# Merge gates by seven half-size products, projections after them, sigmoids and branches kept in DRAM

## The chip, the cores and the metric

The kernel runs on one core of one Trainium2 chip. The metric is device time in microseconds (us) of one execution; the kernel before has a median of 1573.55 us over three runs (1572.86 to 1573.64). The engines of the core are TensorE (PE, matrix products), VectorE (DVE), ScalarE (ACT), GpSimd (POOL) and SyncE (SP); the last two issue the DMAs here.

## What is computed

One layer of a decoder step: 512 prompt rows and 8 sample rows, model width 2048, all in float32. The reference, cut to what bears on the change:

```python
h = rmsnorm(x, norm_in_g) @ w_in          # split into q, k, v, qi, wi, ki, za, u, vb, zb, ga, gb
o_a = sparse attention over the selected keys (prompt_attention, sample_attention)
o_b, vn = gmlp_mix(u, vb, ln_g, ln_b, w_spatial, b_spatial)

def merge_out(x, o_a, z_a, o_b, z_b, g_a, g_b, w_proj_a, w_proj_b, w_out):
    y_a = (o_a * silu(z_a)) @ w_proj_a    # 1024 -> 2048
    y_b = (o_b * silu(z_b)) @ w_proj_b    # 1024 -> 2048
    mix = sigmoid(g_a) * y_a + sigmoid(g_b) * y_b
    return x + mix @ w_out                # 2048 -> 2048
# then a last rmsnorm
```

The gates g_a and g_b are each a product of h (520 x 2048) with 2048 x 2048 weights.

## The kernel before

The rows are kept turned: h is a set of 16 tiles of 128 model columns by T = 520 rows, the first 8 of them the sample rows, and each as two parts, hT_hi and hT_lo, whose sum is the float32 value. A weight is split in the same way: ACT copies it, rounded, to `whi`, and DVE subtracts that from `raw` into `wlo` (`hilo`, L127, whose two operations are at L128 and L84; nearly every DVE instruction bears the line L84 of a counting helper). PE then makes three products a weight tile, hi by hi, hi by lo, and lo by hi.

The unit of the work is a chunk: 1024 weight rows by 128 output columns. `main_chunk` (L269) issues 48 matmuls for it, eight k tiles by three products by two halves of 260 columns (HALF), into one of the two pairs of banks of `psm`, named `pm`. Output blocks over 2048 rows take two chunks, those over 1024 rows (the projections) one. A `raw` tile of 1024 rows by 256 columns (1 MB, three buffers, loaded by SP) serves two column blocks.

The loop at L1474 sets the order on every engine; nothing is reordered afterwards. In iteration i it issues the split of chunk i + 2 (LOOK), then what reads the banks of chunk i - 1 (`pending`), then the matmuls of chunk i, and then one step of every job in the list `jobs` (a job is a generator, and each `yield` ends its step for that iteration). `TT` tiles come from one pool of 37 slots.

Chunks 0 to 91 are indexer, keys, values, and the gMLP branch u, v, z_b. Then follow eight groups of four gate chunks g_b and two chunks of proj_b (92 to 139), q (140 to 155), z_a (156 to 171), gates g_a and proj_a interleaved with four blocks of lead (172 to 219), and w_out (220 to 315). A gate's `evac_g` (L1050) leaves its sigmoid `sg` in a slot, `evac_yb` (L1057) multiplies with it and stores to `mixd` in DRAM, `evac_ya` (L1319) does the same for A and adds the part of B loaded back, and `mix_split` (L1328) splits the sum into hT_hi and hT_lo, which by then no other stage reads. `oa` and `ob` are the split operands of the projections and stay in SBUF. The sample rows of `oa` come from `sample_attend` (L1154), a job of sixteen steps that starts with the last q block (L1087).

Of the kernel before, what the change touches and what calls it, by code (L numbers as in the profile page):

```python
# [38 lines left out]
GA_AHEAD = 4  # L39
NQI = T - P  # L40
WIKI_AT = 4
SEL_AT = 40
COLS_N = NS + 2 * P
# [15 lines left out]
def kernel(  # L59
# [34 lines left out]
    psm = ctx.enter_context(tc.tile_pool(name="psm", bufs=2, space=bass.MemoryType.PSUM))  # L94
    pss = ctx.enter_context(tc.tile_pool(name="pss", bufs=4, space=bass.MemoryType.PSUM))
    ctx.enter_context(tc.manual_schedule())

# [114 lines left out]
    def split_steps(i, pieces):  # L212
# [4 lines left out]
        lo = wspl.tile([P, 8, P], F32R, name="wlo")  # L217
        if ch["rows"]:
# [27 lines left out]
    def rows_chunk(ch):  # L246
        hi, lo = spl_tiles["rows", ch["kq"]]
        c = ch["c"]
        if c is None and ch["first"]:
            state["ps"] = [psm.tile([P, 2, 512], F32, name="pm") for _ in range(2)]  # L250
        elif ch["first"]:
            state["ps"] = SB("rowp")
# [16 lines left out]
    def main_chunk(i, hook=None):  # L269
        ch = chunks[i]  # L270
        if ch["rows"]:
            return rows_chunk(ch)
        if ch["first"]:
            state["ps"] = psm.tile([P, 2, 512], F32, name="pm")
# [13 lines left out]
        return ps  # L288

# [28 lines left out]
    mixd = dram.tile([KT, P, T], F32, name="mixd")  # L318

# [719 lines left out]
    def gate_b(g):  # L1039
# [4 lines left out]
        ob[g] = (TT("obh", (P, T), F32R), TT("obl", (P, T), F32R))  # L1044
        hilo(ob[g][0], ob[g][1], t)
# [30 lines left out]
    def evac_q(h):  # L1076
        def f(ps):
# [8 lines left out]
            if h == 7:  # L1086
                start(sample_attend())  # L1087
# [454 lines left out]
```

## Time and profile before

| | |
|---|---|
| median of three runs | 1573.55 us (1572.86 to 1573.64) |
| the profiled execution, its time | 1568.56 us |
| its span, first to last instruction | 1566.9 us |
| mean granted TensorE clock | 0.996 |
| PE busy | 1531.4 us, 98% |
| DVE busy | 749.3 us, 48% |
| ACT busy | 495.2 us, 32% |
| POOL busy | 262.5 us, 17% |
| DMA | 173.89 MB, mean 111 GB/s |

All rows come from one profiled execution. Busy shares are means over stages with different limits, so a stage is read by the stretch of its own. A row of a timeline gives start, duration, engine, line and operation, the output tile and after `<-` the inputs, and in brackets how long the engine had been idle and what ended that. Matmuls overlap, so the distance of their starts, not their duration, gives the pace.

### The profile page before, as it was taken

The numbers are of one execution on the slowest core, as the hardware profiler recorded it, in microseconds if no ns is written. First come the engines' busy times: TensorE is split into PE (matmuls) and PEld (weight loads), VectorE is DVE, ScalarE is ACT, GpSimd is POOL, SyncE is SP. The second block draws the span as 40 slices with busy tenths as digits, with TensorE's granted clock in tenths as the row PEclk, the third lists the DMA queues.
The fourth block names the chain that finished last, engine by engine and source line by source line (L and its number), as shares of the span: only waits on it lengthen the run. The fifth ranks groups of instructions, "written<-read, shape, count | busy, mean of one in ns | idle before, by whom it ended". The sixth has DMA issues, their size and how long they took to land. (4 is left out here: it accounts for less than half of the span.)

```text
span 1566.9 us, 28327 instructions
## 1 busy us (share of the span) xinstructions
PE 1531.4 (98%) x12222; PEld 1520.4 (97%) x12222; DVE 749.3 (48%) x1550; ACT 495.2 (32%) x803; POOL 262.5 (17%) x324
## 2 busy tenths in 40 slices
PE   5999999999999999999999999999999999999996
PEld 4999999999999999999999999999999999999996
DVE  7545447888998632222222445655223322622324
ACT  6534332433223222222212344334222222422322
POOL 3000007884000220000000002371000000410111
PEclk9999999999999999999999999999999999999998
DMA  6433224447222233332433113345223332633212
GB/s 190 137 115 103 86 88 152 162 129 179 80 83 82 84 108 99 117 95 95 125 117 110 55 55 111 106 145 166 88 89 100 117 122 88 209 99 108 81 55 110
DMA packets 147586, 173.89 MB, mean 111 GB/s; under 512 B 5876, under 2 KB 136300, under 8 KB 147452
## 3 DMA queue, kind: packets, MB, share of 16 engines
q1 hardware_dynamic: 136292, 139.74, 28.6%
q0 software_dynamic: 11168, 32.33, 6.4%
q8 instruction: 96, 1.57, 0.4%
q14 instruction: 30, 0.25, 0.0%
HBM read 162.02 MB, written 10.03 MB: 110 GB/s over the span
## 5 line engine op out<-in xcount | busy, mean ns | idle before, releaser
L285 PE MATMUL pm<-hT_hi,whi 128*128 128x260 f32 (+1 forms) x2736 | 597.4, 291 | 0.0
L285 PE MATMUL pm<-hT_lo,whi 128*128 128x260 f32 (+1 forms) x2736 | 588.7, 289 | 2.4 <-DVE hT_lo L84 2.4
L285 PE MATMUL pm<-hT_hi,wlo 128*128 128x260 f32 (+1 forms) x2720 | 584.1, 289 | 0.0
L84 DVE TENSOR_TENSOR wlo<-raw,whi 128x1024 fp32r<-128x1024 f32 (+2 forms) x260 | 325.6, 1254 | 350.4 <-ACT whi L128 349.6
L285 PEld LDWEIGHTS pm<-hT_lo,whi 128*128 128x128 f32 x2736 | 431.5, 189 | 3.5 <-DVE hT_lo L84 3.2
L285 PEld LDWEIGHTS pm<-hT_hi,whi 128*128 128x128 f32 x2736 | 431.6, 189 | 0.8
L285 PEld LDWEIGHTS pm<-hT_hi,wlo 128*128 128x128 f32 x2720 | 428.3, 189 | 0.0
L128 ACT ACTIVATE whi<-raw 128x1024 fp32r<-128x1024 f32 (+2 forms) x260 | 264.8, 1022 | 321.3 <-PE pm L285 309.9
L263 PE MATMUL pm<-hT_hi,whi 128*128 128x264 f32 x256 | 73.0, 285 | 0.4 <-DVE mixt L84 0.4
L263 PE MATMUL pm<-hT_lo,whi 128*128 128x264 f32 x256 | 73.1, 285 | 0.0
L263 PE MATMUL pm<-hT_hi,wlo 128*128 128x264 f32 x256 | 72.9, 285 | 0.0
L266 PE MATMUL rowp<-whi,hT_hi 128*128 128x256 f32 x256 | 72.7, 284 | 0.0
L266 PE MATMUL rowp<-wlo,hT_hi 128*128 128x256 f32 x256 | 71.9, 281 | 0.0
L266 PE MATMUL rowp<-whi,hT_lo 128*128 128x256 f32 x256 | 71.7, 280 | 0.0
L1053 ACT ACTIVATE sg<-pm 128x520 f32<-128x520 f32 x32 | 19.4, 605 | 152.0 <-PE pm L285 152.0
L1061 POOL DMA_DIRECT2D mixd<-yb x16 | 8.7, 546 | 285.9 <-DVE yb L84 237.7
L1305 POOL DMA_DIRECT2D part<-mixd x16 | 8.6, 541 | 273.8 <-ACT whi L128 220.1
L285 PE MATMUL pm<-obh,wlo 128*128 128x260 f32 x256 | 51.6, 283 | 0.0
L285 PE MATMUL pm<-oah,whi 128*128 128x260 f32 x256 | 51.5, 283 | 0.0
L285 PE MATMUL pm<-obh,whi 128*128 128x260 f32 x256 | 51.5, 283 | 0.0
L285 PE MATMUL pm<-oah,wlo 128*128 128x260 f32 x256 | 51.4, 282 | 0.0
L285 PE MATMUL pm<-oal,whi 128*128 128x260 f32 x256 | 51.4, 282 | 0.0
(462 smaller groups left out, 1920.5 us busy)
## 6 DMA issues: line engine op xcount, KB each, us to landing
raw<-in_w_in_dram SPq DMA_DIRECT2D x91, 1024.0 KB, 5.3
raw<-in_w_out_dram SPq DMA_DIRECT2D x16, 1024.0 KB, 5.4
raw<-in_w_proj_b_dram SPq DMA_DIRECT2D x8, 1024.0 KB, 5.4
raw<-in_w_proj_a_dram SPq DMA_DIRECT2D x8, 1024.0 KB, 5.3
mixd<-yb POOLq DMA_DIRECT2D x16, 260.0 KB, 2.3
part<-mixd POOLq DMA_DIRECT2D x16, 260.0 KB, 3.0
xr<-in_x_prompt_dram POOLq DMA_DIRECT2D x16, 256.0 KB, 6.2
out_dram<-xr SPq DMA_DIRECT2D x16, 256.0 KB, 2.7
```

Source lines behind the costliest of these rows:

```text
L84: return f(out, *a, **k)
L128: nc.scalar.activation(hi, src, AF.Copy)
L263: nc.tensor.matmul(state["ps"][u][:, 0, :COLS_N], lhsT=w[:, k, u * P:(u + 1) * P], rhs=a[:, :COLS_N], **flags)
L266: nc.tensor.matmul(state["ps"][:, :2 * P], lhsT=a[:, off(c):off(c) + P], rhs=w[:, k, :], **flags)
L285: nc.tensor.matmul(ps[:, bank, o:o + t1 - t0], lhsT=w[:, k, :], rhs=a[:, t0:t1], start=(ch["first"] and k == 0 and j == 0), stop=(ch["last ...
L1053: nc.scalar.activation(halves(t), ps[:, :, :HALF], AF.Sigmoid)
L1061: nc.gpsimd.dma_start(mixd[d], t)
L1305: nc.gpsimd.dma_start(part[d], mixd[d])
```

## The change

- The chunks are put in another order: 0 to 91 as before, then q (92 to 107) and z_a (108 to 123), all gates of B and then of A (124 to 235), proj_b (236 to 251), proj_a (252 to 267), w_out (268 to 363).
- A pair of gate column blocks, 2048 weight rows by 256 columns, is cut into four quarters of weights (two row halves by two column halves), h into four quarters (two halves of the 16 tiles by two halves of the 520 rows). Seven products of sums of quarters replace the eight products of quarters. Each product is a chunk of 24 matmuls of 260 columns in a bank of its own (`pone`, four banks). The sums of weight quarters are made in place in `raw` by DVE ahead of the split (`split_steps`), the sums of h quarters once (`build_forms`, forms 3, 5 and 7 in slots, form 6 over a quarter of hT), and the seven results are put together in `seven_after`. The split runs three such chunks ahead (SLOOK).
- The sigmoids are stored to DRAM (`keep_sig`) and loaded two blocks ahead of their use (`load_sig`); `ob` and `oa` are stored to DRAM (`od`) and loaded by `load_o` ahead of their projection.
- `sample_attend` starts with the last seven-product chunk; its end stores the sample rows and then calls `load_o("a", oa)`. `mix_split` goes: `evac_ya` splits its block itself.

On DVE, in the gates, before (`mixt` is a block of proj_a, `part` that of proj_b loaded back):

```order
L84 TENSOR_TENSOR wlo<-raw,whi 128x1024 x5
L84 TENSOR_TENSOR mixt<-pm,sg 128x520
L84 TENSOR_TENSOR mixt<-mixt,part 128x520
L84 TENSOR_TENSOR wlo<-raw,whi 128x1024
L84 TENSOR_TENSOR mixt<-pm,sg 128x520
```

On DVE, in the gates, after: one group of seven (`s_` holds products 1 and 5, `c_` the two output blocks; `raw<-raw` is a sum of two weight quarters):

```order
L85 TENSOR_TENSOR raw<-raw 128x8x128
L85 TENSOR_TENSOR wlo<-raw,whi 128x1024
L85 TENSOR_TENSOR c_9901<-pone,c_9901 128x260
L85 TENSOR_TENSOR raw<-raw 128x8x128
L85 TENSOR_TENSOR wlo<-raw,whi 128x1024
L85 TENSOR_TENSOR s_9900<-pone,s_9900 128x260
L85 TENSOR_TENSOR c_9901<-c_9901,s_9900 128x260
L85 SCALAR_TENSOR_TENSOR c_9902<-c_9902,s_9900 128x520
L85 TENSOR_TENSOR wlo<-raw,whi 128x1024
L85 TENSOR_TENSOR raw<-raw 128x8x128
L85 TENSOR_TENSOR wlo<-raw,whi 128x1024
L85 TENSOR_TENSOR raw<-raw 128x8x128
```

Seven `wlo` in a group stand where four stood in a pair, and four sums of raw halves and the sums of products stand between them.

On DVE, in the last z_a blocks, before (`zs` and `oal` are the sample columns and the remainder of A's operand):

```order
L84 COPY zs<-za 128x8
L84 TENSOR_TENSOR za<-za,oT 128x512
L84 TENSOR_TENSOR oal<-za,oah 128x512
L84 TENSOR_TENSOR wlo<-raw,whi 128x1024 x2
L84 COPY zs<-za 128x8
L84 TENSOR_TENSOR za<-za,oT 128x512
```

The same place after (`x_` are sums of h quarters, `Fh` and `Fl` their two parts):

```order
L85 TENSOR_TENSOR wlo<-raw,whi 128x1024
L85 TENSOR_TENSOR x_8356<-hT_hi 128x520
L85 TENSOR_TENSOR x_8356<-x_8356,hT_lo 128x520 x2
L85 TENSOR_TENSOR Fl<-x_8356,Fh 128x520
L85 SCALAR_TENSOR_TENSOR x_8364<-x_8356,hT_hi 128x520
L85 TENSOR_TENSOR x_8364<-x_8364,hT_lo 128x520
L85 TENSOR_TENSOR wlo<-raw,whi 128x1024
L85 TENSOR_TENSOR x_8424<-hT_hi 128x520
L85 TENSOR_TENSOR x_8424<-x_8424,hT_lo 128x520 x2
L85 TENSOR_TENSOR Fl<-x_8424,Fh 128x520
L85 SCALAR_TENSOR_TENSOR x_8432<-x_8364,hT_hi 128x520
L85 TENSOR_TENSOR x_8432<-x_8432,hT_lo 128x520
```

Six and seven operations for the forms stand between two `wlo` there.

On PE, at the two transposes of sample attention (`soT`), before:

```order
L285 MATMUL pm<-hT_lo,whi 128x260 x2
L285 MATMUL pm<-hT_hi,wlo 128x260 x2
L1285 MATMUL soT<-ident,sos 128x128 x2
L285 MATMUL pm<-hT_hi,whi 128x260 x2
L285 MATMUL pm<-hT_lo,whi 128x260 x2
```

On PE, at the same transposes after (`oh` and `ol` are operands of a projection loaded back; the matmuls above are of chunk 251, the last of proj_b, those below of chunk 252, the first of proj_a):

```order
L353 MATMUL pm<-ol,whi 128x260 x2
L353 MATMUL pm<-oh,wlo 128x260 x2
L1448 MATMUL soT<-ident,sos 128x128 x2
L353 MATMUL pm<-oh,whi 128x260 x2
L353 MATMUL pm<-ol,whi 128x260 x2
```

On POOL's queue after, behind the last sigmoids of that stage (`mso` are the sample columns, `oda` A's operand in DRAM):

```order
L1208 DMA sg<-sigda 128x520
L1468 DMA part<-mixd 128x520
L1208 DMA sg<-sigda 128x520
L1468 DMA part<-mixd 128x520
L1459 DMA oda<-mso 128x8x8 x2
L1214 DMA oh<-oda 128x520
L1214 DMA ol<-oda 128x520
```

The transposes have moved from among matmuls over h to the seam of proj_b and proj_a, and fourteen more loads of the same kind follow on POOL's queue behind the two stores.

The core of the diff:

```diff
+    SEVEN = (1, 5, 7, 3, 2, 4, 6)
...
+            if isinstance(g, dict):
+                r0 = len(raws)
+                for kc in range(2):
+                    raws.append((g["ap"], g["col"], kc, 2 * P))
+                one = {}
+                for step, f in enumerate(SEVEN):
+                    chunks.append(dict(seven=True, rows=False, raw=r0, step=step, f=f, last=True, new=True, group=g, one=one, cuts=((0, HALF, 0, 0),)))
...
+        if ch.get("seven"):
+            spl_tiles[ch["raw"], ch["step"]] = (hi, lo)
+            a, b = raw_tiles[ch["raw"]], raw_tiles[ch["raw"] + 1]
+            b11, b12, b21, b22 = a[:, :, :P], a[:, :, P:], b[:, :, :P], b[:, :, P:]
+            step = ch["step"]
+            if step == 1:
+                add(b11, b11, b12)
+            elif step == 2:
+                add(b12, b12, b22)
+            hilo(hi, lo, (b11, b11, b12, b22, b21, b21, b22)[step])
+            if step == 3:
+                add(b22, b11, b22)
+                load_raw()
+            elif step == 4:
+                add(b21, b22, b21)
+            elif step == 6:
+                del raw_tiles[ch["raw"]], raw_tiles[ch["raw"] + 1]
+                load_raw()
+            return
...
+        if ch.get("seven"):
+            ps = one_bank()
+            out = ps[:, :HALF]
+            hi, lo = spl_tiles.pop((ch["raw"], ch["step"]))
+            for k in range(8):
+                rh, rl = ch["group"]["forms"](ch["f"], k)
+                for j, (w, a) in enumerate(((hi, rh), (hi, rl), (lo, rh))):
+                    nc.tensor.matmul(out, lhsT=w[:, k, :], rhs=a, start=k == 0 and j == 0,
+                                     stop=k == 7 and j == 2)
+            return ps
...
+    def seven_after(ch, ps):
+        g, one, step = ch["group"], ch["one"], ch["step"]
+        out = ps[:, :HALF]
+        if step == 0:
+            one["s"], one["o"] = TT("s15"), [TT("c0"), TT("c1")]
+        s, (o0, o1) = one["s"], one["o"]
+        s1, s5 = s[:, :HALF], s[:, HALF:]
+        if step == 0:
+            nc.scalar.activation(s1, out, AF.Copy)
+        elif step == 1:
+            nc.scalar.activation(s5, out, AF.Copy)
+        elif step == 2:
+            add(o1[:, HALF:], out, s5)
+            nc.scalar.activation(o0[:, HALF:], out, AF.Copy)
+        elif step == 3:
+            add(o1[:, :HALF], out, s5)
+        elif step == 4:
+            add(o0[:, :HALF], out, s1)
+        elif step == 5:
+            add(o0[:, HALF:], out, o0[:, HALF:])
+        else:
+            add(s1, out, s1)
+            add(o0[:, HALF:], o0[:, HALF:], s1)
+            vec.scalar_tensor_tensor(halves(o1), halves(o1), -1.0, s1.unsqueeze(1).to_broadcast([P, 2, HALF]),
+                                     op0=ALU.mult, op1=ALU.subtract)
+            nc.scalar.activation(o0, o0, g["func"])
+            nc.scalar.activation(o1, o1, g["func"])
+            for f, o in zip(g["after"], (o0, o1)):
+                f(o)
...
-    for j in range(0, 16, 2):
-        group(w_in2, C_GB + j * P, KT, rhs_h, [lz("evac_g", ("b", j)), lz("evac_g", ("b", j + 1))])
-        group(w_proj_b[0], j * P, 8, lambda k: ob[k], [lz("evac_yb", j), lz("evac_yb", j + 1)])
...
+    forms = {}
+    for x, col in (("b", C_GB), ("a", C_GA)):
+        for j in range(0, 16, 2):
+            sgroup(w_in2, col + j * P, lambda f, k: forms[f](k), AF.Sigmoid,
+                   [lz("keep_sig", x, j), lz("keep_sig", x, j + 1)])
+    for x, w, o in (("b", w_proj_b[0], ob), ("a", w_proj_a[0], oa)):
+        for j in range(0, 16, 2):
+            group(w, j * P, 8, lambda k, o=o: o[k], [lz("evac_y" + x, j), lz("evac_y" + x, j + 1)])
...
+    def build_forms():
+        A11, A12, A21, A22 = range(4)
+        made, x6s = {}, []
...
+        for k in range(0, 8, 2):
+            (h11, l11), (h12, l12), (h21, l21), (h22, l22) = (
+                (f32(quad(hT_hi, r, k)), f32(quad(hT_lo, r, k))) for r in range(4))
+            x = T2("x5")
+            sub(x, h22, h21)
+            add(x, x, l22)
+            sub(x, x, l21)
+            keep(5, k, x)
+            x6 = T2("x6")
+            vec.scalar_tensor_tensor(x6, x, -1.0, h11, op0=ALU.mult, op1=ALU.subtract)
+            sub(x6, x6, l11)
+            x6s.append(x6)
+            yield
+            x = T2("x7")
+            sub(x, h11, h21)
+            add(x, x, l11)
+            sub(x, x, l21)
+            keep(7, k, x)
+            x = T2("x3")
+            vec.scalar_tensor_tensor(x, x6, -1.0, h12, op0=ALU.mult, op1=ALU.subtract)
+            sub(x, x, l12)
+            keep(3, k, x)
+            yield
+        while state["i"] < first7:
+            yield
+        for k, x6 in zip(range(0, 8, 2), x6s):
+            hilo(quad(hT_hi, A21, k), quad(hT_lo, A21, k), x6)
...
+        o = (TT("obh", (P, T), F32R), TT("obl", (P, T), F32R))
+        hilo(o[0], o[1], t)
+        for m in range(2):
+            nc.gpsimd.dma_start(od["b"][g, m], o[m])
...
+    def keep_sig(x, d):
+        def f(t):
+            nc.gpsimd.dma_start(sigd[x][d], t)
...
+    def load_o(x, o):
+        for k in range(8):
+            o[k] = (TT("oh", (P, T), F32R), TT("ol", (P, T), F32R))
+            for m in range(2):
+                nc.gpsimd.dma_start(o[k][m], od[x][k, m])
...
+            t = sig.pop(("b", d))
+            vec.tensor_tensor(halves(t), ps[:, :, :HALF], halves(t), op=ALU.mult)
             nc.gpsimd.dma_start(mixd[d], t)
+            load_sig("b", d + 2)
+            if d == KT - 2:
+                for a in range(2):
+                    load_sig("a", a)
+                    load_part(a)
...
-            if h == 7:
-                start(sample_attend())
...
-        for h in range(8):
-            hilo(oa[h][0][:, :NS], oa[h][1][:, :NS], ms[:, h, :])
-        V["oa"] = True
+        o = [TT("mso", (P, 8, NS), F32R) for _ in range(2)]
+        hilo(o[0], o[1], ms)
+        for m in range(2):
+            nc.gpsimd.dma_start(od["a"][:, m, :, :NS].rearrange("h p n -> p h n"), o[m])
+        load_o("a", oa)
...
-            t = TT("mixt")
-            vec.tensor_tensor(halves(t), ps[:, :, :HALF], halves(sig.pop(("a", d))), op=ALU.mult)
-            add(t, t, part.pop(d))
-            mix[d] = t
+            t, p = sig.pop(("a", d)), part.pop(d)
+            vec.tensor_tensor(halves(t), ps[:, :, :HALF], halves(t), op=ALU.mult)
+            add(t, t, p)
+            hilo(hT_hi[:, d, :], hT_lo[:, d, :], t)
+            load_sig("a", d + 2)
             load_part(d + 2)
+            if d == XR_AT:
+                start(load_x())
...
-        if i > 1:
-            split(i + LOOK)
+        state["i"] = i
+        seven = chunks[i].get("seven")
+        if not seven:
+            while i > 1 and ahead < i + LOOK:
+                ahead += 1
+                split(ahead)
         for f, a in pending:
             f(*a)
+        while seven and ahead < i + SLOOK:
+            ahead += 1
+            split(ahead)
...
+        if i == first7 - 9:
+            start(build_forms())
+        if i == last7 - 2:
+            load_sig("b", 0)
+            load_sig("b", 1)
+        if i == last7:
+            load_o("b", ob)
+            start(sample_attend())
```

## Rows read from the trace of the kernel before

**Rows 1.** Section 1 of the page: busy us, share of the span, instructions
```profile
PE 1531.4 (98%) x12222; PEld 1520.4 (97%) x12222; DVE 749.3 (48%) x1550; ACT 495.2 (32%) x803; POOL 262.5 (17%) x324
```

**Rows 2.** Busy us by engine in a stretch, PEclk, DMA share, GB/s
```profile
1139.00:1365.00 226.00, 226.00 (x1888) 226.00 (x1886) 76.76 (x85) 55.20 (x66) 18.42 (x35) 1.00 0.37 115
```

**Rows 3.** Timeline of ACT, gates A: start, us, operation, idle before and releaser
```profile
1192.30 0.60 ACT L1053 ACTIVATE sg<-pm 128x520 f32<-128x520 f32 x1 [4.95 <-PE pm L285]
1192.80 1.05 ACT L128 ACTIVATE whi<-raw 128x1024 fp32r<-128x1024 f32 x1
...
1203.84 0.60 ACT L1053 ACTIVATE sg<-pm 128x520 f32<-128x520 f32 x1 [4.94 <-PE pm L285]
```

**Rows 4.** Timeline of DVE, the same stretch
```profile
1193.89 1.22 DVE L84 TENSOR_TENSOR wlo<-raw,whi 128x1024 fp32r<-128x1024 f32 x1 [5.28 <-ACT whi L128]
...
1209.58 0.70 DVE L84 TENSOR_TENSOR mixt<-pm,sg 128x520 f32<-128x520 f32 x1 [2.93 <-PE pm L285]
1210.31 0.70 DVE L84 TENSOR_TENSOR mixt<-mixt,part 128x520 f32<-128x520 f32 x1
1210.93 1.22 DVE L84 TENSOR_TENSOR wlo<-raw,whi 128x1024 fp32r<-128x1024 f32 x1
```

**Rows 5.** Timeline of PE, column pass of w_out
```profile
1368.96 0.28 PE L263 MATMUL pm<-hT_hi,wlo 128*128 128x264 f32 x1
1369.08 0.28 PE L263 MATMUL pm<-hT_hi,whi 128*128 128x264 f32 x1
```

**Rows 6.** Groups by line and form: count, busy us, mean ns, idle before
```profile
L84 DVE TENSOR_TENSOR wlo<-raw,whi 128x1024 fp32r<-128x1024 f32 x246 | 317.6, 1292 | 350.4 <-ACT whi L128 349.6
...
L84 DVE TENSOR_TENSOR xr<-xr,rowp 128x256 f32<-128x256 f32 x16 | 6.7, 417 | 24.6 <-PE rowp L266 24.6
...
L84 DVE SCALAR_TENSOR_TENSOR ql<-pm,qh 128x520 fp32r<-128x520 f32 x8 | 5.6, 700 | 3.6 <-ACT qh L1081 3.1
...
L1375 ACT ACTIVATE of<-pm 128x264 f32<-128x264 f32 x16 | 6.0, 391 | 69.3 <-PE pm L263 69.2
...
L128 ACT ACTIVATE hT_hi<-mixt 128x520 fp32r<-128x520 f32 x16 | 9.2, 628 | 9.4 <-DVE mixt L84 9.3
```

**Rows 7.** Timeline of ACT and DVE, a za pair
```profile
1088.24 0.68 DVE L84 TENSOR_TENSOR za<-za,oT 128x512 f32<-128x512 f32 x1
...
1089.02 0.63 ACT L128 ACTIVATE oah<-za 128x512 fp32r<-128x512 f32 x1 [0.18 <-DVE za L84]
...
1089.68 0.69 DVE L84 TENSOR_TENSOR oal<-za,oah 128x512 fp32r<-128x512 f32 x1 [0.76 <-ACT oah L128]
```

**Rows 8.** Section 6 of the page: DMA issues, KB each, us to landing
```profile
mixd<-yb POOLq DMA_DIRECT2D x16, 260.0 KB, 2.3
part<-mixd POOLq DMA_DIRECT2D x16, 260.0 KB, 3.0
```

**Rows 9.** Busy us by engine in a stretch with a full queue
```profile
1364.00:1368.00 4.00, 3.57 (x30) 3.36 (x29) 2.10 (x3) 1.57 (x2) 2.05 (x4) 1.00 1.01 362
```

**Rows 10.** Timeline of PE and DVE, end of sample attention
```profile
1094.03 0.38 PE L1285 MATMUL soT<-ident,sos 128*128 128x128 f32 x2
...
1095.10 0.32 DVE L84 TENSOR_TENSOR ms<-so,zs 128x32 f32<-128x32 f32 x2
```

**Rows 11.** Section 5 of the page: POOL issuing loads
```profile
L1305 POOL DMA_DIRECT2D part<-mixd x16 | 8.6, 541 | 273.8 <-ACT whi L128 220.1
```

**Rows 12.** DMA issues with short runs, KB, us to landing
```profile
srd<-ssc POOLq DMA_DIRECT2D x1, 64.0 KB, 15.3
```

**Rows 13.** Timeline of PE at the start of the program
```profile
28.47 0.52 PE L285 MATMUL pm<-hT_hi,wlo 128*128 128x392 f32 x1
...
29.52 0.34 PE L285 MATMUL pm<-hT_hi,wlo 128*128 128x392 f32 x1
```

**Rows 14.** Busy us by engine at the end of the program
```profile
1558.00:1562.00 4.00, 0.00 (x0) 0.00 (x0) 1.58 (x6) 1.33 (x2) 0.00 (x0) 0.50 0.92 348
```

More of the change, by code (lines that the diff above doesn't have):

```diff
@@ L38 @@
 LOOK = 2
-GA_AHEAD = 4
+SLOOK = 3
 NQI = T - P
@@ L42 @@
 SEL_AT = 40
+XR_AT = 8
 COLS_N = NS + 2 * P
@@ L93, with banks, pair_banks, one_bank @@
     dram = ctx.enter_context(tc.tile_pool(name="scratch", bufs=1, space=bass.MemoryType.DRAM))
-    psm = ctx.enter_context(tc.tile_pool(name="psm", bufs=2, space=bass.MemoryType.PSUM))
     pss = ctx.enter_context(tc.tile_pool(name="pss", bufs=4, space=bass.MemoryType.PSUM))
     ctx.enter_context(tc.manual_schedule())
+    mains = {}
+    def banks(kind):
+        if mains.get("kind") == kind:
+            return
+        if "cm" in mains:
+            mains["cm"].__exit__(None, None, None)
+        mains["n"] = mains.get("n", 0) + 1
+        cm = tc.tile_pool(name=f"psm{mains['n']}", bufs=2 if kind == "pair" else 4, space=bass.MemoryType.PSUM)
+        mains.update(kind=kind, cm=cm, pool=cm.__enter__())
+    def pair_banks():
+        banks("pair")
+        return mains["pool"].tile([P, 2, 512], F32, name="pm")
+    def one_bank():
+        banks("one")
+        return mains["pool"].tile([P, 512], F32, name="pone")
     xp = x_prompt[0]
@@ L249, in rows_chunk @@
         if c is None and ch["first"]:
-            state["ps"] = [psm.tile([P, 2, 512], F32, name="pm") for _ in range(2)]
+            state["ps"] = [pair_banks() for _ in range(2)]
         elif ch["first"]:
@@ L318 @@
     mixd = dram.tile([KT, P, T], F32, name="mixd")
+    sigd = {x: dram.tile([KT, P, T], F32, name="sigd" + x) for x in "ab"}
+    od = {x: dram.tile([8, 2, P, T], F32R, name="od" + x) for x in "ab"}
     evacs_of = {}
@@ L361, with quad, T2, keep @@
     build()
+    rows_first = [i for i, ch in enumerate(chunks) if ch["rows"]][0]
+    first7 = [i for i, ch in enumerate(chunks) if ch.get("seven")][0]
+    last7 = [i for i, ch in enumerate(chunks) if ch.get("seven")][-1]
+    def quad(t, r, k, n=2):
+        return t[:, (r % 2) * 8 + k:(r % 2) * 8 + k + n, (r // 2) * HALF:(r // 2 + 1) * HALF]
+    def build_forms():
+        A11, A12, A21, A22 = range(4)
+        made, x6s = {}, []
+        for f, r in ((1, A11), (2, A12), (4, A22), (6, A21)):
+            forms[f] = lambda k, r=r: tuple(quad(t, r, k, 1)[:, 0, :] for t in (hT_hi, hT_lo))
+        def T2(name, dt=F32):
+            return TT(name, (P, 2, HALF), dt)
+        def keep(f, k, x):
+            made[f, k] = (T2("Fh", F32R), T2("Fl", F32R))
+            hilo(*made[f, k], x)
+        for f in (3, 5, 7):
+            forms[f] = lambda k, f=f: tuple(t[:, k % 2, :] for t in made[f, k - k % 2])
+        for k in range(0, 8, 2):
[25 more added lines that the diff above has]
+            hilo(quad(hT_hi, A21, k), quad(hT_lo, A21, k), x6)
     sqw = const.tile([1, 1], F32, name="sqw")
@@ L1350, in load_x @@
         for q in range(4):
+            if q == 2:
+                while state["i"] < rows_first:
+                    yield
             xr["g", q] = TT("gf", (P, 512))
@@ L1482 @@
         if ch["last"]:
-            if not ch["rows"]:
+            if seven:
+                pending.append((seven_after, (ch, ps)))
+            elif not ch["rows"]:
                 pending.append((ch["evac"], (ps,)))
```

66 lines of the change are left out of this document (18 added, 48 removed).

## The prediction, made before the run

> **What bounds the kernel now.** Read first the share of each engine [rows 1]: TensorE (PE) is busy 98% of the span, VectorE (DVE) 48%, ScalarE (ACT) 32%. Then the same by stage [rows 2]: over the merge gates of A with proj_a, 1139 to 1365 us, PE is busy all 226.00 us at a granted clock of 1.00, DVE 76.76. So here time is PE's stream of matmuls, and removing some shortens the span, if what feeds PE keeps up. The pace: two sigmoids of one gate pair start 11.54 us apart (1192.30, 1203.84) [rows 3], and two chunks of 48 matmuls lie between them: 0.1202 us a matmul, 5.77 us a chunk, 23.08 us for a pair of gate column blocks in four chunks. Third, the timelines of ACT and DVE [rows 3, 4]: a weight block costs a 1.05 us copy on ACT (whi), then 1.22 us on DVE (wlo), which starts 0.04 after the copy ends, and DVE had stood idle 5.28 before it. That idle time is what the change uses.
>
> **What is removed.** Sixteen pairs of gate blocks take 7 x 24 matmuls in place of 4 x 48: 24 fewer each, 384 in all, 46.2 us at 0.1202. Each half chunk of 24 uses fresh weights at every matmul; in w_out the weights change at each matmul already, and matmuls of 264 columns follow each other in 0.12 us [rows 5], so I charge nothing for that. PE would need 20.2 us a group.
>
> **What the steady group costs on DVE and ACT.** Seven blocks are split, not four, and the order of the program is fixed on each engine. From single rows I walk one group on DVE. Prices: wlo 1.22, 1.14 where the next is independent (1210.31 + 0.70 overlaps the wlo at 1210.93 by 0.08) [rows 4]; a sum of two raw halves, also 128 x 1024, 1.22; a sum of 260 columns 0.34 to 0.45, from 0.417 for 256 [rows 6] with or without that overlap; the one signed sum of 520, 0.70 [rows 6].
> - DVE's own work from one wlo to the next: 1.48 (wlo, a sum of 260), twice 2.70 (wlo, such a sum, a raw sum), 2.63 (wlo, two such sums, the signed one), 2.39 and 2.47 (wlo, a raw sum), 1.56 (wlo, a sum): 15.93 us.
> - Waits. Three raw sums stand just ahead of the split that needs them: DVE sums, ACT needs 0.10 to start, as from the za product to its copy [rows 7], and 1.055 to copy, DVE 0.04 to go on, 1.195 each time with nothing else for DVE in program order. One whi stands behind the second sigmoid, which waits for DVE's signed sum: 0.10, 0.53 (0.60 without the overlap with the next [rows 3]), 1.055 and 0.04, 1.73. One stands behind a product's copy on ACT, which comes after DVE's sum on the same bank: 0.10, 0.29 (0.39 [rows 6] less 0.10 of overlap), 1.055 and 0.04, 1.48. Together 6.80.
>
> Sum 22.73 us, above PE's 20.2 and just under the old 23.08. The look-ahead of three half chunks buys a head start, but cannot help when every group is longer on DVE. So of 46.2 us only 16 x 0.35 = **5.6, say 5.3 us**, are left (the first group partly differs). If each round trip could be hidden, PE would bind and all 46.2 come back; if the eleven operations of 1024 took the 1.29 that wlo takes on the mean of the whole program [rows 6], a group would be 0.8 longer and the term +7. Its bounds are -46 and +7.
>
> **Entry into the seven products.** Over the last eight chunks of za the forms of h are built: 13 operations of 520 columns for two k tiles, three of them behind an ACT copy. At 0.70, with a dependent one 0.03 later [rows 4] and an independent one 0.08 sooner, and 0.77 for each copy (0.63 [rows 6, 7] and two hand-overs), an iteration with x5 takes 6.0 us of DVE, wlo included; one with x7 and x3 and the za chain (product 0.68, copy 0.63, remainder 0.69 [rows 7]) 10.0. Four pairs take 64.0 us from chunk 115 on, while PE has nine chunks, 51.9. The first seven-product chunk needs its banks, which are those of the last za pair, and that pair's silu is queued on ACT behind a whi that waits for DVE. So PE stands **12.1 us**. Ends: 0, if DVE's work overlaps better than a row by row walk, and 18 (four times the excess of 4.45) with no slack at all.
>
> **Into proj_b.** Its 16 operand tiles and two sigmoids come back from DRAM, requested at the last seven-product chunk: 18 loads of 260 KB. A load lands 3.0 us after its issue when alone [rows 8]; at the 362 GB/s of a full queue [rows 9] one takes 0.72, all 13. They can be issued early, as tiles come free some 14 us ahead. The last group's sums stand before the first pair bank: 0.6 us. I take 0.6, ends 0 and 8.
>
> **Into proj_a.** This is the term that decides. Before, sample attention started in the q stage and ended at 1095 us [rows 10], well ahead of the first proj_a block, its operands kept in SBUF. Now it starts at the end of the gates, takes one step an iteration, sixteen in all, so its last step is issued with the last chunk of proj_b. Only that step writes the eight sample columns to DRAM, and only behind it stand the 16 operand loads which the very next chunk needs. On the way: two transposes and DVE work, whose ms products stood 1.07 us behind the transposes in before [rows 10], and with the split and hand-overs I put 2 us; two stores of 128 partitions x 8 x 8, 1024 runs of 32 bytes each; 16 loads at 0.54 us of issue [rows 11] and 0.72 of transfer [rows 9].
> The trace has no such store. Below it stands the 260 KB store of long runs, 2.3 us [rows 8]; above, the store in 4096 runs of 16 bytes, 15.3 us [rows 12]. I take 5.5 for the first (2.3 and a quarter of the difference to 15.3, for a quarter of the runs) and 3.5 for the second behind it.
> The Trainium skill, page "DMA: Bandwidth & Descriptors", section "Anatomy of one DMA — SWDGE (gpsimd) path", gives a fixed 2.0 us and the bytes at 436 GB/s whatever the runs' length: 2.1 us for 32 KB, so by it the two stores together would cost some 6 us less. [rows 12] speaks against it, with 64 KB in 15.3.
> Then the loads: 16 x 0.72 = 11.5, and 2.3 for the last one's landing, less the chunk's own 5.77, which PE works off as tiles arrive. 2 + 9 + 11.5 + 2.3 - 5.8 = 19 us without work for PE. PE then starts slow: at the program's start matmuls came 0.33 us apart up to 28.47 and 0.17 apart from 29.52 [rows 13], after PE had done little; 2.85 us were lost there, and PE's first matmuls here wait for loads anyway, so I count 2. Together **21 us**, ends 12 (store 2.3, no restart) and 31 (store 15.3). In before none of it waited.
>
> **Stores of sigmoids and operands.** Some 64 stores and 64 loads of 260 KB more on POOL's queue, 34 MB; those not counted above are requested two blocks (four chunks, 23 us) ahead of their use, or have stages of hundreds of us to land, and the DMA share is 0.37 there [rows 2]. I charge nothing; without that cover, a load late by 1 us in half of the 32 blocks of proj_b and proj_a would be 16 us.
>
> **The sum.** -5.3 + 12.1 + 0.6 + 21 = +28.4 us on the profiled execution's 1568.56: 1597. The median of the runs is 1573.55, 5.0 above that execution, so I forecast **1602 us**.
>
> **Rivals.**
> 1. *PE stays the bound in the gates.* If ACT and DVE overlap as the idle times of [rows 3, 4] suggest (DVE half idle), a group takes 20.2 and the stage gives 46.2 back; entry and proj_a cost the same 33.7: 12.5 faster, 1561. For it: DVE's own 15.93 is under 20.2. Against it: the five waits follow from the order of instructions. Its point: with 33.7 of other costs the kernel is not slower from a group of 20.97 us down (23.08 - 33.7/16). Chance 0.13.
> 2. *The chain binds, but the hand-overs cost little*: the forms fit into DVE's idle time and the stores are quick, so that proj_a waits under 5 us: 1573.55 - 5.3 + 4 = 1572. Against it: the 16 loads alone need 11.5 for a chunk of 5.77. Chance 0.06.
> 3. *The clock.* PE waits in each group for 2.5 of 22.7 us, in up to seven pieces. If that made the array fall to 1.2 GHz, 168 matmuls would take 40.4 us a group, 16 x 17.7 = 283 more: 1885. In before, the clock was granted at 0.50 with no matmul at all (1558 to 1562) [rows 14], and 1.00 in a stretch with PE busy 3.57 of 4.00 [rows 9]. Chance 0.02. The Trainium skill, page "TensorE: Matmul & The Clock Gate", section "What's actually happening", says that the throttled state is the default and activity releases it; [rows 9, 14] agree, and by it this rival's 1885 would need the gaps to count as rest.
>
> **Chances and range.** The forecast, slower by entry and proj_a: 0.79; the rivals 0.13, 0.06 and 0.02. A measurement of this kernel can tell 0.2%, 3.1 us, from no change. Faster takes rival 1, 0.13, and 0.01 of rival 2: 0.14. Same takes the rest of rival 2 and the low edge of the forecast: 0.06. Slower 0.80. By the terms' ends the forecast alone runs from 1582 (entry 6, proj_a 12, gates -10) to 1622 (gates +5, entry 15, proj_a 27). The range goes from 1568, leaving out rival 1, to 1624.
>
> **What will show it.** In the seven-product stage: wlo of equal steps some 22.7 us apart, PE's share near 0.89, PE idle put down to wlo, and wlo's idle to ACT's whi. A pitch of 20.2 with PE at 1.00 makes rival 1. At the entry: one PE gap near 12 us, released by ACT's za or by DVE. At proj_a: one PE gap of about 19 us, released by loads of oh and ol, and a store of mso whose landing is the size of the gap's first part. No gap there means that sample attention ended earlier than I read. A granted clock of 0.50 through the gates would make rival 3.

## The result, and the profile after

The changed kernel takes 1607.84 us (median of four, 1607.26 to 1613.49) against 1573.6; the ratio is 1.0225, with a 95% interval of 1.0202 to 1.0249. It is slower by 34 us; 1602 was forecast.

The profiled execution is the slowest of the four, with 1613.49 us and a span of 1611.7. First its page, engine shares and granted clock (answering to [rows 1]):

```profile
PE 1518.8 (94%) x11838; PEld 1491.9 (93%) x11838; DVE 961.5 (60%) x1823; ACT 563.2 (35%) x906; POOL 334.6 (21%) x454
...
PEclk9999999999999999999989999999998979999999
```

PE has 384 instructions fewer and is busy for less, but its share fell from 98% to 94%, and the clock dips in three places. What lies there is read by stages. Before that, one thing is set aside. These are windows of the z_b and q stage (us, busy time by engine, PEclk, DMA share, GB/s):

```profile
556.00:560.00 4.00, 2.34 (x13) 2.19 (x13) 0.00 (x0) 0.00 (x0) 1.95 (x3) 0.82 0.03 2
560.00:564.00 4.00, 3.87 (x26) 3.86 (x26) 2.25 (x3) 3.02 (x4) 1.16 (x2) 0.76 0.11 36
```

From 544 to 564 us PE starts 112 matmuls where the kernel before, with the same instructions there, starts 166: 6.5 us lost at 0.1202 a matmul, with no releaser shown. The profiles of the eleven variants below, with the same instructions up to there, start 156 to 166, so they lose 1.2 us at most. The stall is about the 5.6 us by which this execution stands above the other three, which have no profile, so it is taken to be no effect of the change.

**Gates.** ACT's copy of the first product, once in each of 16 groups, by tile (count, ns min/median/max, first and last start), and the stretch 900 to 1000 (answering to [rows 2]):

```profile
L367 ACT ACTIVATE s<-pone x16: 365/368/371, 825.9 to 1164.3; 128x260 f32<-128x260 f32 x16
```

```profile
900.00:1000.00 100.00, 94.92 (x751) 91.35 (x752) 70.35 (x81) 39.98 (x52) 4.34 (x8) 1.00 0.36 117
```

(1164.3 - 825.9)/15 = 22.56 us a group, where 22.73 was walked out row by row; the stage, 815.58 to 1177.68, takes 362.1 us for 369.3 before. The timeline of DVE over part of a group, with PE's longest wait in it, shows why:

```profile
1001.34 1.23 DVE L85 TENSOR_TENSOR wlo<-raw,whi 128x1024 fp32r<-128x1024 f32 x1 [1.21 <-ACT whi L147]
...
1005.63 1.22 DVE L85 TENSOR_TENSOR wlo<-raw,whi 128x1024 fp32r<-128x1024 f32 x1 [1.65 <-ACT whi L147]
1006.89 1.22 DVE L85 TENSOR_TENSOR raw<-raw 128x1024 f32<-128x1024 f32 x1
1006.91 0.39 PE L338 MATMUL pone<-Fh,wlo 128*128 128x260 f32 x1 [0.75 <-DVE wlo L85]
1008.03 1.22 DVE L85 TENSOR_TENSOR wlo<-raw,whi 128x1024 fp32r<-128x1024 f32 x1
1009.28 1.22 DVE L85 TENSOR_TENSOR raw<-raw 128x1024 f32<-128x1024 f32 x1
1011.97 1.23 DVE L85 TENSOR_TENSOR wlo<-raw,whi 128x1024 fp32r<-128x1024 f32 x1 [1.47 <-ACT whi L147]
```

Behind the sum at 1009.28 DVE stands idle 1.47 us for ACT's copy; behind the second sigmoid 1.65. Both engines have time to spare, and the pair of them is the bound. PE waits for the result three times a group, 0.76 us at most. (Its busy share of 94.92 counts spans that overlap; by the pace, 20.2 of 22.56 us, it works 0.90 of the time.)

**Entry.** The timeline at the first product chunk, three engines:

```profile
812.73 1.22 DVE L85 TENSOR_TENSOR raw<-raw 128x1024 f32<-128x1024 f32 x1
...
813.98 1.06 ACT L147 ACTIVATE whi<-raw 128x1024 fp32r<-128x1024 f32 x1 [1.89 <-DVE raw L85]
814.94 0.59 ACT L1300 ACTIVATE za<-pm 128x520 f32<-128x520 f32 x1
...
815.58 0.58 PE L338 MATMUL pone<-hT_hi,whi 128*128 128x260 f32 x1 [11.29 <-ACT za L1300]
```

The chain is the one that was named: DVE, late by the forms, sums; ACT copies; only then comes the silu that frees the banks. 11.29 us, forecast 12.1.

**Entry of proj_b.** Not forecast beyond 0.6 us:

```profile
1180.20 1.06 ACT L147 ACTIVATE whi<-raw 128x1024 fp32r<-128x1024 f32 x1 [4.86 <-DMA raw<-in_w_proj_b_dram]
...
1181.29 1.23 DVE L85 TENSOR_TENSOR wlo<-raw,whi 128x1024 fp32r<-128x1024 f32 x1 [3.29 <-ACT whi L147]
1182.43 0.42 DVE L85 TENSOR_TENSOR s<-pone,s 128x260 f32<-128x260 f32 x1
...
1182.95 0.77 PE L353 MATMUL pm<-oh,whi 128*128 128x260 f32 x2 [5.28 <-issue]
```

Weights of proj_b, loading beside 18 operand loads, land late; DVE's split of them stands ahead of the last product's sum, and that sum frees the bank. (The releaser is read from the times here, 1182.43 + 0.42 against 1182.95; e10 tests it.)

**Inside proj_b.** PE meets the sample's products `ssP`, which wait for `kTl` of POOL:

```profile
1224.97 0.27 PE L1375 MATMUL ssP<-kTl,qsd 128*64 128x128 f32 x1 [1.85 <-POOL kTl L1385]
...
1231.61 0.58 POOL L1332 DMA_DIRECT2D vn<-vd  x1 [3.00 <-DMA mixd<-sg]
...
1235.90 1.31 POOL L1385 TENSOR_TENSOR kTl<-kTs,kTh 128x512 fp32r<-128x512 f32 x1
...
1237.26 0.28 PE L1375 MATMUL ssP<-kTl,qsd 128*64 128x128 f32 x1 [4.56 <-POOL kTl L1385]
```

POOL issues all the new DMAs and also does this arithmetic, in one order. Its own wait of 3.00 us is for a store of `mixd` to land; `vn` takes no data from that store, so what it waits for must be the slot of the common pool that the store holds. PE is idle 10.7 us in the stage. Before, these products cost 2.2 us of waits, of which this is the longest:

```profile
1035.42 0.27 PE L1212 MATMUL ssP<-kTl,qsd 128*64 128x128 f32 x1 [1.50 <-POOL kTl L1222]
```

**Proj_a.** The seam:

```profile
1301.76 0.19 DVE L85 COPY so<-soT 128x32 f32<-128x32 f32 x1 [6.23 <-PE soT L1448]
...
1303.12 0.23 DVE L85 TENSOR_TENSOR mso<-ms,mso 128x64 fp32r<-128x64 f32 x1 [0.38 <-ACT mso L147]
...
1303.38 1.82 POOL L1459 DMA_DIRECT2D oda<-mso  x2 [4.88 <-ACT mso L147]
1306.48 0.57 POOL L1214 DMA_DIRECT2D oh<-oda  x1 [1.28 <-DMA oda<-mso]
...
1309.99 0.77 PE L353 MATMUL pm<-oh,whi 128*128 128x260 f32 x2 [8.26 <-DMA oh<-oda]
...
1313.74 0.59 PE L353 MATMUL pm<-ol,whi 128*128 128x260 f32 x1 [2.98 <-DMA ol<-oda]
```

The chain is as forecast, but the two stores took 3.1 us from the first issue (1303.38) to the load that waits for them (1306.48), not 9. The 9 came from the store of [rows 12]; that one was issued 3 us behind eight loads of 256 KB on the same queue, and two weight loads beside it took twice their median (DMA view of the kernel before, 373 to 389 us, then the whole program):

```profile
raw<-in_w_in_dram SPq DMA_DIRECT2D x2, 1024.0 KB, 10.3
...
raw<-in_w_in_dram SPq DMA_DIRECT2D x91, 1024.0 KB, 5.3
```

From the transposes to w_out the stage takes 110.7 us, 18.4 over the 92.3 of its matmuls: 12.7 idle, the rest nearly all at half clock. The clock in windows at the entry, in the gates and here:

```profile
812.00:816.00 4.00, 0.42 (x2) 0.42 (x3) 2.76 (x3) 1.63 (x3) 1.07 (x2) 0.50 0.42 131
816.00:820.00 4.00, 4.00 (x20) 4.00 (x20) 2.88 (x4) 2.54 (x4) 0.00 (x0) 0.50 0.02 4
...
824.00:828.00 4.00, 4.00 (x36) 4.00 (x35) 2.71 (x6) 2.13 (x4) 1.07 (x2) 1.00 0.88 295
...
1316.00:1320.00 4.00, 4.00 (x21) 4.00 (x20) 0.00 (x0) 0.00 (x0) 3.22 (x6) 0.54 1.30 394
```

20 and 21 matmuls in 4 us at a granted clock of 0.50 and 0.54, where 36 stand in a window at 1.00: behind a gap of some us PE works on at 1.2 GHz for a while before it is back at 2.4. With half of PE's busy time at 0.50 counted as lost, an estimate, that makes 3 us behind the entry, 5.6 in proj_b (1.7 in the kernel before, at its sample attention) and 5 in proj_a.

**The sum**, on the spans (1611.7 - 1566.9 = 44.8): the stall at 550 us 6.5, gates -7.2 (with 3 of slow clock in them), entry 11.3, entry of proj_b 5.3, waits in proj_b 10.7 - 2.2 = 8.5 and some 4 of slow clock, proj_a 18.4, w_out to the end 199.8 for 202.1, -2.3: 44.5. Under half a us is not placed.

### The profile page after: what moved, and what is told of

Same layout as the page of the kernel before. It is cut to its first block, busy times and chain, and to the rows that moved or that the text cites. A ratio compares the mean times of both kernels' runs of the same rounds, so it can differ in the third digit from the quotient of the medians.

```text
span 1611.7 us, 28326 instructions
## 1 busy us (share of the span) xinstructions
PE 1518.8 (94%) x11838; PEld 1491.9 (93%) x11838; DVE 961.5 (60%) x1823; ACT 563.2 (35%) x906; POOL 334.6 (21%) x454
## 4 chain that ended last, share of the span: by engine, by line
PE 46%; issue 39%; POOL 5%; DVE 4%; DMA 3%; ACT 1%; SPq 0%; POOLq 0%; ACTq 0%; DVEq 0%
PE pm L353 31%; PE pm L321 6%; PE rowp L324 5%; DVE vr L85 1%; PE ssp L837 1%; POOL ridx L1015 1%; DMA ol<-oda 1%; DMA sg<-sigdb 1%; DVE wlo L85 1%; POOL kg L1326 1%; POOL sigda L1202 1%; DMA mixd<-sg 1%; POOL oda L1312 1%; PE ixp L133 1%; PE ixp L134 1%
## 5 line engine op out<-in xcount | busy, mean ns | idle before, releaser
L353 PE MATMUL pm<-hT_hi,whi 128*128 128x260 f32 (+1 forms) x1712 | 391.0, 297 | 0.8 <-issue 0.8
L353 PE MATMUL pm<-hT_lo,whi 128*128 128x260 f32 (+1 forms) x1712 | 383.6, 293 | 3.1 <-DVE hT_lo L85 2.4
L353 PE MATMUL pm<-hT_hi,wlo 128*128 128x260 f32 (+1 forms) x1696 | 379.1, 293 | 2.0 <-issue 2.0
L353 PEld LDWEIGHTS pm<-hT_lo,whi 128*128 128x128 f32 x1712 | 274.2, 189 | 4.5 <-DVE hT_lo L85 3.2
L353 PEld LDWEIGHTS pm<-hT_hi,whi 128*128 128x128 f32 x1712 | 274.2, 190 | 1.4 <-issue 0.8
L353 PEld LDWEIGHTS pm<-hT_hi,wlo 128*128 128x128 f32 x1696 | 271.1, 189 | 3.0 <-issue 3.0
L338 PE MATMUL pone<-hT_hi,whi 128*128 128x260 f32 x512 | 145.7, 285 | 11.3 <-ACT za L1300 11.3
L338 PE MATMUL pone<-hT_hi,wlo 128*128 128x260 f32 x512 | 148.7, 290 | 0.8 <-DVE wlo L85 0.3
L338 PE MATMUL pone<-hT_lo,whi 128*128 128x260 f32 x512 | 145.8, 285 | 0.0
L338 PE MATMUL pone<-Fh,wlo 128*128 128x260 f32 x384 | 111.7, 291 | 16.7 <-DVE wlo L85 16.7
```

What stands on the lines that cost most here:

```text
L338: nc.tensor.matmul(out, lhsT=w[:, k, :], rhs=a, start=k == 0 and j == 0, stop=k == 7 and j == 2)
L353: nc.tensor.matmul(ps[:, bank, o:o + t1 - t0], lhsT=w[:, k, :], rhs=a[:, t0:t1], start=(ch["first"] and k == 0 and j == 0), stop=(ch["last ...
```

## The experiments

Times are compared with the kernel before run on the same chip; its median was 1574.2 for the first four, 1574.9 for e5 to e7, 1567.9 for e8 and e9, 1574.1 for the last two. The theory has four parts: the order of DVE and ACT in the gates; the forms at the entry; sample attention and operand loads at proj_b; the seam to proj_a. The main rival is that PE, or the mere amount of DVE work, sets the pace of seven products. Profiles of one program differ by stage: e8 turned out to be the changed kernel again, and its proj_b is 2 us shorter, so a smaller difference of one stage shows nothing.

**e1, sums one split early.**

```diff
-    SEVEN = (1, 5, 7, 3, 2, 4, 6)
+    SEVEN = (1, 3, 5, 7, 2, 6, 4)
...
-            if step == 1:
+            hilo(hi, lo, (b11, b22, b11, b12, b21, b22, b21)[step])
+            if step == 0:
                 add(b11, b11, b12)
-            elif step == 2:
+            elif step == 1:
                 add(b12, b12, b22)
-            hilo(hi, lo, (b11, b11, b12, b22, b21, b21, b22)[step])
-            if step == 3:
+            elif step == 2:
                 add(b22, b11, b22)
```

> The changed kernel with the same DVE work per group, but each sum of raw weight quarters stands one split earlier, behind a split that does not need it (the seven products run in the order 1, 3, 5, 7, 2, 6, 4). Theory: the group of seven takes 22.6 us because DVE waits for ACT's copy behind each of its own sums; with another split in between the wait is filled, PE binds, the pitch of a group is 20.2 us and its product chunks leave no PE gap over 0.4 us. 16 x 2.4 = 38 us less: about 1570 us. Rival 1, the amount of DVE work sets the pace, not its order: pitch stays 22.6, time about 1608. Rival 2, PE itself is slower with fresh weights at each matmul: pitch 22.6 with PE busy throughout.

The rest of the edit follows from the new order of products: they are joined one step ahead of the sigmoids, and ACT makes one more copy of 260 columns a group. 1565.43 us; ratio 0.9939 (0.992 to 0.9958), 0.6% faster than the kernel before. By tile, in the same stretch, and PE at proj_b's first product:

```profile
L368 ACT ACTIVATE s<-pone x16: 362/367/370, 818.6 to 1118.2; 128x260 f32<-128x260 f32 x16
```

```profile
900.00:1000.00 100.00, 100.00 (x838) 100.00 (x838) 78.74 (x90) 47.03 (x65) 5.35 (x10) 1.00 0.39 132
...
1134.96 0.48 PE L354 MATMUL pm<-oh,whi 128*128 128x260 f32 x2 [1.07 <-issue]
```

19.97 us a group, PE busy throughout, with the same sums and splits on DVE (its share even rises, as more groups fit in). Both rivals fall: the order of the same work was the cost. The gates take 324.3 us, 38 less; the rest of the 42 us comes mainly at proj_b, whose first gap is 1.07 for 5.28 us with the same 18 loads beside it.

**e2, proj_a's operands without the sample columns.** In their place silu(z_a) is stored with the rest, so attention is missing from the sample rows.

```diff
-        load_o("a", oa)            # end of sample_attend
...
+        if i == last7 + 16:
+            load_o("a", oa)
```

> The changed kernel with the operands of proj_a loaded back without the sample columns that sample attention makes (silu of z_a stands in their place, so the sample rows of the output leave attention out): the 16 loads are issued right behind the last chunk of proj_b, ahead of the transposes and the two stores, which still run. Theory: of the 18.4 us that proj_a's stage is longer, only what lies between the transposes and the first load's issue (4.9 us) belongs to the sample columns, the rest to reloading 16 tiles at once and to PE's restart at half clock: 5 us less, about 1603, with a PE gap of some 3.5 us and then waits on single loads. Rival, the wait for sample attention is the whole of it: the gap goes, 18 us less, about 1590.

1601.71 us, 1.0169 (1.0145 to 1.0193). Timeline of PE at the seam:

```profile
1298.57 0.36 PE L353 MATMUL pm<-oh,whi 128*128 128x260 f32 x1 [1.63 <-DVE mso L85]
```

From the transposes to w_out 103 us for 110.7: 7.6 less (6.1 in the time), so the sample columns hold two fifths of the 18.4 and the reload with its slow restart the rest; these two were not taken apart. The theory's 5 was somewhat low, the rival's 18 wrong.

**e3, forms over 16 chunks**: start at `first7 - 17`, two `yield`s for one.

> The changed kernel with the forms of h built over the last 16 chunks ahead of the seven products, one step every second chunk, in place of the last 8. Theory: the gap of 11.3 us at the entry is DVE's excess of 4.45 us over each two chunks of z_a; spread over twice the time DVE needs about 10.5 of each 11.54 us, so the gap goes, and with it PE's restart at half clock (2 to 3 us): 13 to 14 us less, about 1594. Rival, the gap is the hand-over of the banks from pairs to single ones and of the last z_a to ACT: it stays, time about 1608.

1601.79 us, 1.0164 (1.0139 to 1.0189): half of what was expected. PE in the timeline:

```profile
720.46 0.30 PE L1278 MATMUL tA<-ident,pB 128*128 128x128 f32 x1 [4.43 <-DVE pB L85]
...
806.63 0.39 PE L338 MATMUL pone<-hT_hi,whi 128*128 128x260 f32 x1 [0.69 <-ACT za L1302]
```

The entry's gap goes, as the theory has it; but the first forms now stand on DVE ahead of the last heads' softmax, PE waits 4.43 us there, and restarts slow. In e6 and its kin the forms start two chunks later, and neither gap is above 0.7 us.

**e4, the new order with plain gates**: `sgroup(...)` replaced by `group(w_in2, col + j * P, KT, rhs_h, [evac_g ...])`, no forms built, sigmoids still to DRAM.

> The new order of chunks and the sigmoids and operands kept in DRAM, but the gates by four plain chunks of 48 matmuls a pair, without forms and seven products. Theory: 384 matmuls come back (gates 369 us, 7 more than the 362 measured), the entry gap with its restart goes (11.3 + 2.9 less), and the costs of proj_b and proj_a stay as they are (some 37 us over the pace of their matmuls): about 1601, that is, 27 over the kernel before although not one product is changed. Rival, the order and DRAM are free and the loss is in the seven products: about 1574.

1597.92 us, 1.0149 (1.0122 to 1.0175). So the order and the detour by DRAM alone cost 24 us, 27 having been expected; the seven products with their forms add the remaining 10, so in this form the 384 matmuls saved bring nothing.

**e5, kTl on DVE**: `nc.gpsimd.tensor_tensor(yl, t, f32(yh), op=ALU.subtract)` becomes `sub(yl, t, f32(yh))`.

> The changed kernel with one operation moved: the remainder kTl of the sample's keys is made by DVE and not by POOL. Theory: in proj_b PE stands behind the products ssP for about 10.5 us, and 3.5 more go to the restart at half clock, because kTl stands on POOL behind DMA issues (stores of mixd that wait for DVE, loads of sigmoids, gathers); on DVE, which is half idle there, it comes at once: the PE waits released by kTl go, 10 to 13 us less, about 1596. Rival, the gathers themselves land late, so kTs is late whoever makes kTl: the waits stay with another releaser, time about 1606.

1603.98 us, 1.0177 (1.016 to 1.0194). Proj_b takes 114.4 us for 118.8 (116.7 in e8), a third of the expected gain at most. DVE and PE:

```profile
1223.05 0.45 DVE L85 COPY_PREDICATED kg<-newm,kn 128x256 f32<-128x256 int32 x1
...
1228.62 0.71 DVE L85 STREAM_TRANSPOSE kTs<-kg 128x512 f32<-128x512 f32 x1 [5.12 <-DMA mixd<-sg]
...
1230.04 0.37 PE L1375 MATMUL ssP<-kTh,qsd 128*64 128x128 f32 x1 [3.96 <-ACT kTh L1384]
```

As the rival has it, the longest wait stays with another releaser, but not because a gather lands late: the gathered `kg` is in use at 1223.05, and `kTs` then waits 5.12 us for a store of `mixd`, from which it takes no data. So it waits for that store's slot in the common pool. No run changes the size of the pool or the slots of these stores, so how much of proj_b's waits this makes is not shown.

**e8 and e10, the last sums ahead of the split.** e8 issued the pending sums ahead of the split at proj_b's first chunk; e10 also caps the look-ahead:

```diff
-        while seven and ahead < i + SLOOK:
+        while seven and ahead < min(i + SLOOK, last7 + 2):
```

> The changed kernel with one swap, at the first chunk of proj_b: the sums and sigmoids of the last product are issued ahead of the split of chunk 238, not behind it. Theory: PE's gap of 5.3 us there ends with the product's sum (s<-pone,s at 1182.43), which frees the bank of the first pair; on DVE it stands behind a wlo whose raw weights landed late (1180.2) among 18 operand loads. Moved ahead of it, the sum can run at 1178.0, the gap shrinks to under 1.5 us and PE is not slowed behind it: 5 to 6 us less, about 1602. Rival, PE waits for the operands oh and ol themselves: the gap stays at 5 us and the time at 1608.

> What e8_sums_before_split meant to do and did not, since the split of chunk 238 is issued one iteration earlier, with the last product: here the last product's iteration splits up to chunk 237 only, so that on DVE the last sums stand ahead of the wlo of chunk 238. Theory: the first pair's bank comes free at the end of the product's sum, some 0.5 us behind the last product, and PE's gap of 5.2 us shrinks to under 1.5 us, with PE at its full clock behind it: 5 to 6 us less than the changed kernel, ratio to the kernel before 1.019. Rival, the operands oh and ol are late as well: the gap stays above 4 us, then released by their loads, ratio 1.0225.

e8 left DVE's order as it was (that split is issued one iteration earlier), and measured 1.0233 (1.0219 to 1.0247), the changed kernel again. e10: 1605.82 us, 1.0199 (1.0185 to 1.0213).

```profile
1172.23 0.42 DVE L85 TENSOR_TENSOR s<-pone,s 128x260 f32<-128x260 f32 x1
...
1172.75 0.36 PE L353 MATMUL pm<-oh,whi 128*128 128x260 f32 x1 [0.75 <-issue]
```

The gap of 5.2 us is 0.75, so the bank was its cause; but from the last product to proj_a's seam the stage is only 1.2 us shorter (120.6 for 121.9 in e8): single operand loads now hold PE for 2.1 us, where in e8 they held it for none, and some other waits grow too. The ratio is 1.0199 where 1.019 was expected, and its interval overlaps that of the changed kernel. Both readings were half right.

**e6, e7, e9 and e11, all mended.** The sums as in e1, forms at chunks 109 to 122, kTl on DVE, sample attention started some product chunks before the last and some pairs of proj_a's operands loaded as soon as it ends (e9 also has the swap of e8):

```diff
+        if i == last7 - 4:
+            start(sample_attend())
+        if i == last7 + 16:
+            load_o("a", oa, range(6, 8))
...
+        load_o("a", oa, range(6))  # end of sample_attend
```

> Sums one split early (as in e1_sums_early), forms of h at chunks 109 to 122, kTl on DVE, sample attention started four product chunks earlier, and six of eight pairs of proj_a's operands loaded as soon as its end has stored the sample columns, the last two behind the last chunk of proj_b. Theory, taking the costs as separate: from 1565 for the sums alone, 9 less at the entry, 10 to 12 less in proj_b, 14 to 16 less at proj_a: about 1530, 2.8% under the kernel before, with no PE gap over 3 us between 800 us and w_out. Rival, the waits are one chain of DVE and POOL work that only moves: 1550 or more, with new gaps in z_a or proj_b.

> As e6_all_mended, but sample attention starts two product chunks earlier than in the changed kernel and four of eight pairs are loaded early. Theory: the loads that remain for the seam are eight of 0.72 us, about the length of one chunk, so little is lost against e6: 0 to 4 us more than e6. Rival, what counts is the time at which sample attention ends: the seam shows a wait of several us again.

> As e6_all_mended, with four pairs of proj_a's operands loaded early in place of six, and the swap of e8_sums_before_split. Theory: e6's gap of 4.43 us at the seam comes from sigmoid loads that stand on POOL behind early loads without a free slot; with fewer early loads it goes, while 8 loads of 0.72 us remain for the seam, and the entry of proj_b keeps its two gaps, which are sample attention's first products ahead of the operands: 1543 to 1549. Rival, the number of early loads does not matter, since the slots come free only with the last chunk of proj_b: the gap stays, 1547.

> As e6_all_mended, with sample attention started nine product chunks before the last product in place of four. Theory: e6's gaps of 8.8 and 7.0 us at the entry of proj_b come from the sample's products, which stand in PE's order ahead of proj_b and wait for gathers that share the queue with 18 operand loads; five chunks (14 us) earlier the gathers land before these loads start, the gaps shrink to under 4 us together, and the time is 8 to 12 us less than e6, a ratio of 0.975. Rival, the slots of the pool are full of the forms of h, so the gathers wait for the same slots: the gaps stay or move into the last gates, ratio 0.982 or more.

| | chunks early, pairs early | us | ratio (95%) |
|---|---|---|---|
| e6 | 4, 6 | 1547.28 | 0.9822 (0.9806 to 0.9838) |
| e7 | 2, 4 | 1554.59 | 0.9861 (0.9845 to 0.9877) |
| e9 | 4, 4 | 1551.19 | 0.9896 (0.9881 to 0.9911) |
| e11 | 9, 6 | 1552.34 | 0.9855 (0.984 to 0.987) |

The ratio is what compares, since the kernel before took 1567.9 us beside e9. e6 beats both kernels, 1.8% under the one before, but is 17 us short of the expected 1530. Its timeline, PE and DVE:

```profile
1122.03 6.37 DVE L85 CAST qsd<-qsl 32x64 fp32r<-32x64 f32 x32 [3.84 <-POOL qsd L1358]
...
1130.43 0.34 PE L1383 MATMUL ssP<-kTh,qsd 128*64 128x128 f32 x1 [8.83 <-ACT kTh L1392]
...
1141.55 0.56 PE L354 MATMUL pm<-oh,whi 128*128 128x260 f32 x1 [6.99 <-issue]
...
1241.73 0.70 DVE L85 TENSOR_TENSOR sg<-pm,sg 128x520 f32<-128x520 f32 x1 [12.96 <-DMA sg<-sigdb]
...
1242.57 0.77 PE L354 MATMUL pm<-oh,whi 128*128 128x260 f32 x2 [4.44 <-DVE sg L85]
```

The rival's view holds for the seams: the waits moved. Started early, sample attention stands on DVE in the way of the entry of proj_b: its 32 small casts take 6.37 us behind a POOL memset, `kTh`, for which PE waits 8.83 us, comes only after them, and later steps of it (1136 to 1141 us) stand ahead of the sum that frees proj_b's first bank. One step is issued in each iteration, and an iteration of a half chunk is half as long. Loaded early, proj_a's operands stand on POOL ahead of a sigmoid load. e7, with both less early, loses 7 us on e6 where 0 to 4 were expected, and waits 4.13 us at the seam, as its rival had it. Four pairs (e9) shrink the wait of 4.44 to 2.92 us and bring 2.64 back later; nine chunks (e11) put a gap of 7.5 into the last gates, behind the same casts and not behind late gathers, and 6.6 at the seam. Each expected more than it gave.

## Why the prediction was right

- *Gates*, forecast -5.3, measured -7.2: the walk over DVE's order gave 22.73 us a group, the trace 22.56, and e1 shows, with the same sums and splits in another order, that the order was the cause. The rival of a PE bound (20.2) was the pace after e1, not before it. Of the signs named, PE's share near 0.89 is met by the pace, not by the busy time.
- *Entry*, 12.1 and 11.3, by the chain that was named; e3 removes it by moving the forms.
- *Proj_a*, 21 and 18.4, from two errors that largely cancel, which is luck. The restart: 2 us forecast, 5.7 measured. The stores: 9 us forecast from the row of 16-byte runs [rows 12], 3.1 measured. That row was taken as a price of short runs, but its store ran beside other loads, and how much of its 15.3 us is due to the runs and how much to these loads is not shown. The Trainium skill ("DMA: Bandwidth & Descriptors", "Anatomy of one DMA — SWDGE (gpsimd) path") has a fixed 2.0 us and a term for the bytes alone; the estimate from it, 2.1 us a store, was nearer to the 3.1 for both than that row.
- *Proj_b* is the step that failed: 0.6 us were put down and sample attention was charged only for its end. It cost 5.3 at the entry (inside the ends of that term, 0 and 8), and 8.5 of waits with some 4 of slow clock, for which there was no term at all. In the kernel before, POOL's queue carried little but sample attention's own gathers at that time (its packets took 21.5% of the DMA engines' time from 1000 to 1040 us); now it also carries stores and loads of 260 KB (41.5% from 1177 to 1243 us). The working counted the last step of sample attention but not the other fifteen. How these waits divide between POOL's order, full queues and the pool's slots stays open.
- *The clock*: rival 3, a fall in the gates, did not come: 1.00 at a PE share of 94.92 in 100 [as in the row above]. But each gap of several us elsewhere was followed by a stretch at 1.2 GHz, charged once and paid four times.

Without its stall the profiled execution stands 38.3 us of span over the one before, where 28.4 were summed: proj_b is +17 of the difference, gates, entry, proj_a and w_out together -8. The medians are only 34.2 apart, 5.8 over the forecast, because the execution profiled before ran 5 us under its median. So the direction was right, and so were the mechanisms of the gates, the entry and the seam; that 1602 lies so near is partly luck, since 17 us that were left out met 8 that were charged too high and those 5.

## What to carry to other kernels

When work is shaved off the bounding engine, walk the next engines instruction by instruction in program order: two engines that both have time to spare can bind together, if each waits for the other in turn, and putting independent work between producer and consumer gave back 38 us with the same sums and splits. When a stage is moved, count every step of it against the queue it lands beside, and against the buffers it shares with what else stands there, not only its last. Before a row is used as a price, look at what else moved beside it. And a gap of several us on TensorE cost more than its length each time here.

## What the hardware showed that was not expected

- Two stores of 128 x 8 x 8 in 32-byte runs land within 3.1 us of the first issue, with nothing else on the DMA engines; a 64 KB store in 16-byte runs took 15.3 us [rows 12] beside other loads.
- From 822 to 1177 us PE was idle three times in each group, 0.76 us at most, and the granted clock stayed at 1.00.
- One execution lost 6.5 us at 550 us without a releaser in the trace; the same instructions lost 1.2 us at most in other profiles. What it was is open.
